# Token routing of a mixture-of-experts block: a written order for three engines, filler products, one product for the shift columns, and the last expert pairs without lag

## The chip, the cores and the metric

The kernel runs on one core of one Trainium2 chip. The metric is the device time of one execution in microseconds; the median of several runs is given. The engines that matter are TensorE (PE for products, PEld for its weight loads), VectorE (DVE), ScalarE (ACT), GpSimd (POOL) and SyncE (SP), which issues nearly all transfers from HBM.

## The reference, cut to what matters

The program computes one diffusion-transformer block (gated delta rule and dilated attention, then a mixture of experts) and two more layers (differential attention and a short convolution, each with an MLP) for 256 tokens of width 1024 in float32. The change touches the mixture of experts and what stands just ahead of it:

```python
h2 = _rms(x, g_ffn) * (1.0 + sc2) + sh2
scores = sigmoid(h2 @ w_router)                       # 256 x 64
sel = scores + router_bias
grp_score = sum of the two best sel of each of 8 groups; the 4 best groups stay
_, eidx = top_k(where(emask, sel, -inf), 8)           # 8 of 64 experts per token
wk = scores[eidx] / sum(scores[eidx]) * 2.5
routed = sum over experts e of (silu(h2 @ w_gate[e]) * (h2 @ w_up[e]) * wk[e]) @ w_down[e]
x = x + gt2 * (routed + shared expert)
```

Each expert has three weight arrays of 1 MB (1024x256, 1024x256, 256x1024); all 64 and the shared one are read.

## The kernel before

Phase A ends with the mixers' up-projections and w_out, whose output tiles arrive one 128-channel tile `f` at a time. `before_b` prepares what routing needs; among it the shift `sh2`, which lies as 8 columns of `self.mod` and is wanted in `self.shc` in another arrangement (channel p*8+j in row p, column j). It makes a row of 1024 values by 8 products with one column of weights (`ps_shr`, L904) and two copies on ScalarE (L905), and turns that row by 8 products with one row of weights (`ps_shc`, L909). `router` then splits the router weights and multiplies the shift with them (`ps_shl`, L923).

`ahead` runs once for each channel tile as soon as w_out has made it: a split in a rounded high part and a low part on ScalarE and VectorE (`xgh`, `xgl`), squares for the norm, then the router's products (`ps_r`) and transposes of the scaled tile (`ps_x`). `rows` follows the last tile: the norm factor `tr` (a power on GpSimd), the scores `th` (L1013), their tanh (L1015), and the token rows of h2 in high and low part, `h2th` (ScalarE, L1021) and `h2tl` (VectorE, L1022), four pieces each.

`route` finds each token's mask of 8 experts by a chain of VectorE instructions (`sel` L1031 to `mask` L1053) and ranks the tokens of each expert by products (`ps_rk`, L1059 and L1060). `order` counts tokens per expert, sorts experts by count (`key`, `rank`, `perm`), makes the list `ids` of experts in that order, the combine weights `cmb`, and `rks`/`cms`, ranks and weights in that order. The first 8 experts (N_FIX) are fixed, so the first pairs can start before the order is known.

Experts are worked off in "quads" of two units (a unit: two experts with 64 token slots each, or one with 128, or four with 32). For a quad, `places` makes one-hot matrices P on VectorE, `gather` makes the slots' inputs X from h2 (L1259, four steps, evicted by ScalarE at L1261), `weigh` makes the combine weights (L1275), `hidden` multiplies with gate and up weights (L1296), `gated` applies silu, `turned` transposes, `down` multiplies with the down weights (L1334), and `scatter` adds the result to the residual (L1349). The loop in `phase_b` runs these over 15 quads with a lag: in the turn of quad q it gathers q+1, multiplies q-1 with its down weights, and scatters q-2.

Weights come through SP into rings: 11 buffers of 1 MB in `ring2`, 4 in `ring`, and 3 in `ring4` for the start; a load waits until its buffer's last reader is done. Eighteen loads are issued ahead of routing.

The order of instructions on an engine comes from the planner of the language, by its own costs, except inside `tc.manual_schedule(engines=...)`: there the named engines keep the order of the program text. Before the change, only TensorE is so fixed, in the first gather and in the loop.

Of the kernel before, what the change touches and what calls it, by code (L numbers as in the profile page):

```python
# [10 lines left out]
F32 = mybir.dt.float32  # L11
# [7 lines left out]
T = 256  # L19
# [24 lines left out]
C_N = C_GRP + 24  # L44
B_SLOT, B_KEY, B_RANK, B_BASE, B_SH, B_MEM, B_COL, B_GRP = (
    c - C_SLOT for c in (C_SLOT, C_KEY, C_RANK, C_BASE, C_SH, C_MEM, C_COL, C_GRP))
# [22 lines left out]
N_WARM = 10  # L69


def make_consts():
# [44 lines left out]
class Kern:  # L117
# [231 lines left out]
    def phase_a(self):  # L349
        nc, tc, a, cst = self.nc, self.tc, self.a, self.cst  # L350
        with ExitStack() as st:
# [158 lines left out]
            for u in range(4):  # L510
                def sink(ft, ps, u=u):
                    f = u * 2 + ft
                    nc.vector.scalar_tensor_tensor(xT[:, f, :T], ps, gt[:, f:f + 1], xT[:, f, :T],
                                                   op0=ALU.mult, op1=ALU.add)
# [367 lines left out]
    def before_b(self):  # L882
# [78 lines left out]
    def ahead(self, j, sp):  # L961
# [6 lines left out]
        x = self.xT[:, j, :T]  # L968
        hi, lo = (sp.tile([128, T], F32R, tag=n, name=n, bufs=1) for n in ("xgh", "xgl"))
# [3 lines left out]
        sq = sp.tile([128, T], F32, tag="sqx" if j else "sqs", name="sqx", bufs=1)  # L973
        nc.scalar.activation(sq, x, AF.Square)
# [6 lines left out]
        yield  # L981

# [4 lines left out]
        if j == KC - 1:  # L987
# [1018 lines left out]
```

## Time and profile before

| | |
|---|---|
| median of 3 runs | 1699.44 us (1698.04 to 1704.7) |
| profiled execution, its own time | 1702.65 us |
| its span, first to last instruction | 1700.6 us |
| mean granted TensorE clock | 0.972 of full speed |
| TensorE busy | 1616.6 us, 95% of the span |
| VectorE, ScalarE, GpSimd busy | 956.6, 678.8, 136.4 us |
| HBM read | 388.85 MB |

Busy shares are averages over stages with different limits. The router's stage starts near 534 us of the span, the expert loop near 554, and the second block near 1039.

### The profile page before, as it was taken

How to read it: one execution, taken by the hardware profiler on the slowest of the kernel's cores; microseconds unless marked ns; L12 is line 12 of the kernel's file. 1: busy time of each engine (PE TensorE's matmuls, PEld its weight loads, DVE VectorE, ACT ScalarE, POOL GpSimd, SP SyncE). 2: the span in 40 equal slices, each digit the busy share in tenths (PEclk: the TensorE clock that was granted, in tenths of full speed). 3: DMA queues.
4: the chain of work that ended last, by engine and by line, in shares of the span. 5: the costliest groups of instructions: out<-in, count | busy, mean ns of one | idle time of the engine just before them, and what ended most of it. 6: DMA issues, size and time to landing. Idle time of an engine off the chain costs nothing. (4 is left out here: it accounts for less than half of the span.)

```text
span 1700.6 us, 31649 instructions
## 1 busy us (share of the span) xinstructions
PE 1616.6 (95%) x12857; PEld 1421.0 (84%) x12857; DVE 956.6 (56%) x2068; ACT 678.8 (40%) x1355; POOL 136.4 (8%) x120
## 2 busy tenths in 40 slices
PE   6999999999997999989999997999899999989998
PEld 3899999999997656756776655888899999989998
DVE  5779796976276132322243335675865447686543
ACT  4434334334444221222132213555554345465532
POOL 0121212122100000000000001011100010010000
PEclk8899999999998999999999998999899999989999
DMA  9535442555279599999999995423455554545552
GB/s 312 193 111 174 127 144 79 166 181 174 82 248 412 230 412 420 419 419 419 418 416 390 419 419 170 141 78 100 149 181 189 176 174 149 162 145 183 191 176 75
DMA packets 198496, 391.97 MB, mean 230 GB/s; under 512 B 8760, under 2 KB 158908, under 8 KB 173260
## 3 DMA queue, kind: packets, MB, share of 16 engines
q1 hardware_dynamic: 197916, 389.69, 62.9%
q8 instruction: 102, 1.67, 0.4%
q10 hardware_dynamic: 432, 0.23, 0.1%
q14 instruction: 46, 0.38, 0.1%
HBM read 388.85 MB, written 1.05 MB: 229 GB/s over the span
## 5 line engine op out<-in xcount | busy, mean ns | idle before, releaser
L148 ACT ACTIVATE hi<-w 128x1024 fp32r<-128x1024 f32 (+3 forms) x316 | 314.8, 1003 | 350.6 <-PE proj L167 248.7
L152 DVE TENSOR_TENSOR lo<-w,hi 128x1024 fp32r<-128x1024 f32 (+3 forms) x287 | 328.8, 1150 | 172.6 <-ACT hi L148 159.5
L1296 PE MATMUL ps_gu<-w,X 128*64 128x256 f32 (+2 forms) x2112 | 222.2, 388 | 11.9 <-DMA w<-in_w_exp_up 11.4
L1296 PEld LDWEIGHTS ps_gu<-w,X 128*64 128x64 f32 (+2 forms) x2112 | 145.7, 134 | 91.5 <-issue 16.0
L166 PE MATMUL proj<-hsh,hi 128*128 128x258 f32 (+2 forms) x824 | 208.5, 289 | 0.0
L167 PE MATMUL proj<-hsl,hi 128*128 128x258 f32 (+2 forms) x824 | 206.2, 285 | 0.0
L166 PE MATMUL proj<-hh,hi 128*128 128x256 f32 x640 | 168.2, 296 | 0.6 <-DVE cv L604 0.6
L167 PE MATMUL proj<-hl,hi 128*128 128x256 f32 x640 | 166.1, 292 | 0.1
L166 PEld LDWEIGHTS proj<-hsh,hi 128*128 128x128 f32 x824 | 156.9, 190 | 1.8 <-issue 1.1
L167 PEld LDWEIGHTS proj<-hsl,hi 128*128 128x128 f32 x824 | 157.7, 191 | 0.1
L152 POOL TENSOR_TENSOR lo<-w,hi 128x1024 fp32r<-128x1024 f32 x29 | 70.2, 2423 | 929.3 <-ACT hi L148 879.0
L1304 DVE SCALAR_TENSOR_TENSOR tg<-tg,ps_gu 128x256 f32<-128x256 f32 x30 | 12.6, 421 | 201.7 <-ACT tg L1303 201.7
L166 PEld LDWEIGHTS proj<-hh,hi 128*128 128x128 f32 x640 | 123.8, 193 | 1.9 <-issue 0.7
L167 PEld LDWEIGHTS proj<-hl,hi 128*128 128x128 f32 x640 | 123.6, 193 | 0.8 <-DVE hl L421 0.3
L169 PE MATMUL proj<-hsh,lo 128*128 128x258 f32 (+2 forms) x824 | 115.8, 283 | 0.0
L1334 PE MATMUL ps_d<-w,hT 128*64 128x512 f32 (+2 forms) x528 | 112.0, 597 | 0.7 <-DMA w<-in_w_exp_down 0.7
L169 PEld LDWEIGHTS proj<-hsh,lo 128*128 128x128 f32 x824 | 106.5, 189 | 0.0
L169 PE MATMUL proj<-hh,lo 128*128 128x256 f32 x640 | 102.8, 293 | 0.0
L1303 ACT ACTIVATE tg<-ps_gu 128x256 f32<-128x256 f32 x30 | 11.5, 384 | 215.8 <-PE ps_gu L1296 215.8
L166 PE MATMUL proj<-oh,hi 128*128 128x258 f32 (+1 forms) x384 | 96.2, 285 | 0.4 <-ACT oh L1939 0.4
L167 PE MATMUL proj<-ol,hi 128*128 128x258 f32 (+1 forms) x384 | 95.2, 283 | 0.0
L1334 PEld LDWEIGHTS ps_d<-w,hT 128*64 128x64 f32 (+2 forms) x528 | 34.4, 131 | 67.0 <-issue 46.2
(488 smaller groups left out, 3239.0 us busy)
## 6 DMA issues: line engine op xcount, KB each, us to landing
w<-in_w_in SPq DMA_DIRECT2D x66, 1024.0 KB, 5.1
w<-in_w_exp_up SPq DMA_DIRECT2D x64, 1024.0 KB, 17.7
w<-in_w_exp_gate SPq DMA_DIRECT2D x64, 1024.0 KB, 18.8
w<-in_w_exp_down SPq DMA_DIRECT2D x64, 1024.0 KB, 19.8
w<-in_w_up SPq DMA_DIRECT2D x32, 1024.0 KB, 5.5
w<-in_w_down SPq DMA_DIRECT2D x32, 1024.0 KB, 5.2
w<-in_w_ada SPq DMA_DIRECT2D x24, 1024.0 KB, 5.5
w<-in_w_out SPq DMA_DIRECT2D x8, 768.0 KB, 4.4
```

Source lines behind the costliest of these rows:

```text
L148: nc.scalar.activation(hi, v, AF.Copy)
L152: eng.tensor_tensor(lo, v, hi.bitcast(F32), op=ALU.subtract)
L166: nc.tensor.matmul(ps, wh(j), xh(j), start=(first and j == 0), stop=False)
L167: nc.tensor.matmul(ps, wh(j), xl(j), start=False, stop=False)
L169: self.last_mm = nc.tensor.matmul(ps, wl(j), xh(j), start=False, stop=(last and j == n - 1))
L1296: nc.tensor.matmul(ps[b0:b1, c * 256:c * 256 + 256], Q.X[:, j, n * 128 + b0:n * 128 + b1], w[:, j, :], start=(j == 0), stop=(j == KC - 1))
L1303: nc.scalar.activation(tg, ps[:, 0:256], AF.Tanh, scale=0.5)
L1304: nc.vector.scalar_tensor_tensor(tg, tg, 1.0, ps[:, 0:256], op0=ALU.add, op1=ALU.mult)
L1334: nc.tensor.matmul(psd[hf][b0:b1, :], hT[:, f, b0:b1], v[i][:, f, halves[hf]], start=(f == 0), stop=(f == 1))
```

## The change

It has five parts.

- **Shift columns by one product.** `before_b` multiplies, on VectorE, a constant pattern with the 8 shift columns (each broadcast over 16 columns) and turns the result by one product with a second constant pattern into `ps_shc`.
- **Written order of three engines.** `in_order` fixes TensorE, VectorE and ScalarE to the order of the text for the last channel tile, `rows`, `route`, the first steps of `order` and the first gather. That text is rearranged: squares and their products first in `ahead`; in `rows` the tanh after two of the four high parts, and only one of the four low parts there; two low parts ahead of `places` and one behind it.
- **Filler products.** Ten products of 128x128 with 128x256 into a bank that nothing reads, ahead of the ranking products.
- **Route in steps around gather.** `order` is a generator: its counting products come ahead of the places, its VectorE chain behind the first step of the gather, the `ids`, `sT` and `ps_end` products behind the gather, and the slot products behind the first `hidden`. `weigh` and `gated` of the first unit come ahead of the second `hidden`, `places` of the next quad too. In every turn `weigh` of the next quad now stands behind its `gather`, not between its steps. The banks of `pg` and `pgu` change sides with those of `pm`, `pd` and `py`; `PT` has 3 buffers in place of 4, `tg` one in place of 2.
- **Last pairs without lag.** In the turn before the last, the quad of that turn is turned, multiplied with its down weights, and its predecessor scattered, so that in the last turn only one scatter and the last quad's own work are left.

```diff
+    out[:, C_TURN:C_TURN + 128] = p // 8 == i % 16
+    out[:, C_TURN + 128:C_TURN + 136] = p % 8 == np.arange(8)[None, :]
...
                     f = u * 2 + ft
-                    nc.vector.scalar_tensor_tensor(xT[:, f, :T], ps, gt[:, f:f + 1], xT[:, f, :T], op0=ALU.mult, op1=ALU.add)
-                    yield from self.ahead(f, wk)
+                    with self.in_order(f == KC - 1):
+                        nc.vector.scalar_tensor_tensor(xT[:, f, :T], ps, gt[:, f:f + 1], xT[:, f, :T], op0=ALU.mult, op1=ALU.add)
+                        ahead = self.ahead(f, wk)
+                        next(ahead)
+                    yield
+                    with self.in_order(f == KC - 1):
+                        list(ahead)
...
-            self.rows()
+            with self.in_order():
+                self.rows()
+    def in_order(self, so=True):
+        E = mybir.EngineType
+        return self.tc.manual_schedule(engines={E.PE, E.DVE, E.Activation}) if so else nullcontext()
...
-        row = self.ring.tile([128, 2048], F32, tag="w", name="w")[0:1, 0:D]
-        for hf in range(2):
-            ps = self.pm.tile([128, 512], F32, tag="m", name="ps_shr")
-            for j in range(4):
-                c = 24 + hf * 4 + j
-                nc.tensor.matmul(ps[0:1, j * 128:j * 128 + 128], self.mod[:, c:c + 1], self.ident, start=True, stop=True)
-            nc.scalar.activation(row[:, hf * 512:hf * 512 + 512], ps[0:1, :], AF.Copy)
+        turn = self.ring.tile([128, 2048], F32, tag="w", name="w")[:, 0:128]
+        nc.vector.tensor_tensor(turn.rearrange("p (j i) -> p j i", j=8), self.CB[:, B_TURN:B_TURN + 128]...,
+                                self.mod[:, 24:32].unsqueeze(2).to_broadcast([128, 8, 16]), op=ALU.mult)
         ps = self.pm.tile([128, 512], F32, tag="m", name="ps_shc")
-        vs = row.rearrange("o (p j) -> o j p", j=KC)
-        for j in range(KC):
-            nc.tensor.matmul(ps[:, j:j + 1], vs[:, j, :], self.ones[0:1, 0:1], start=True, stop=True)
+        nc.tensor.matmul(ps[:, 0:KC], turn, self.CB[:, B_TURN + 128:B_TURN + 136], start=True, stop=True)
...
     def rows(self):
+        def part(n, lo): ...                      # one of the four pieces of h2th (lo False) or h2tl (lo True)
+        part(0, False)
+        part(1, False)
         nc.scalar.activation(self.th, self.th, AF.Tanh, scale=0.5)
-        for t in range(2):
-            for hf in range(2): ...               # h2th and h2tl, piece by piece
+        part(2, False)
+        part(3, False)
+        part(0, True)
+        self.low_parts = lambda ns: [part(n, True) for n in ns]
...
     def route(self, tok, sp):
+        psw = pm.tile([128, 512], F32, tag="m", name="ps_w")
+        for _ in range(N_IDLE):                   # 10
+            nc.tensor.matmul(psw[:, 0:256], self.ident, self.C[:, 0:256], start=True, stop=True)
...
     def phase_b(self):
+            with self.in_order():
+                psk = self.route(self.tok, self.sp)
+                order = self.order(self.tok, self.sp)
+                next(order)                       # counting products
+                first = self.quad(psk[:, :, E_FIX:], None, units[0:2], wk)
+                self.low_parts((1, 2))
                 self.places(first, self.slm)
-                list(self.gather(first))
-            self.order(self.tok, self.sp)
+                self.low_parts((3,))
+                gs = self.gather(first)
+                next(gs)
+                next(order)                       # rk, key, rank, perm, cmb, cmf, cnt, room, extra
+                list(gs)
+                next(order)                       # ps_ids, sT, ps_end
...
                     self.hidden(Q, 0)
-                    if q:
-                        self.gated(Q, 0)
+                    if q == 0:
+                        list(order)               # slot products, rks, cms
+                        list(self.weigh(Q))
+                    self.gated(Q, 0)
+                    if nxt:
+                        self.places(nxt)
+                    else:
+                        list(self.scatter([old.out[n] for n in range(2)]))
                     self.hidden(Q, 1)
+                    self.gated(Q, 1)
+                    if not nxt:
+                        break
                     for i in range(4):
                         next(ys, None)
-                        next(ws, None)
-                        next(gs, None)
                         if i > 1 and old:
                             self.turned(old, i - 2)
+                        next(gs)
                     list(ys)
                     list(gs)
                     list(ws)
                     if old:
                         self.down(old, 0, wo)
                         self.down(old, 1, wo)
-                for i in range(2):
-                    self.turned(Q, i)
-                list(self.scatter([old.out[n] for n in range(2)]))
+                    if q == nq - 2:
+                        for i in range(2):
+                            self.turned(Q, i)
+                        list(self.scatter([old.out[n] for n in range(2)]))
+                        self.down(Q, 0, wo)
+                        self.down(Q, 1, wo)
+                self.turned(Q, 0)
                 self.down(Q, 0, wo)
+                self.turned(Q, 1)
                 list(self.scatter([Q.out[0]]))
                 self.down(Q, 1, wo, True)
                 list(self.scatter([Q.out[1]]))
```

## Rows read from the trace of the kernel before

**Rows 1.** Windows of the expert stage: stretch, length, busy of each engine, clock, transfers.
```profile
553.50:561.50 8.00, 8.00 (x64) 5.14 (x65) 1.09 (x6) 1.62 (x5) 0.00 (x0) 1.00 0.08 19
...
575.50:585.50 10.00, 10.00 (x76) 8.07 (x78) 1.07 (x6) 2.74 (x7) 0.00 (x0) 0.83 0.06 13
585.50:1021.00 435.50, 421.25 (x3408) 281.30 (x3404) 139.19 (x352) 97.69 (x214) 0.00 (x0) 0.99 1.01 415
```

**Rows 2.** Timeline of SP's transfers: start, duration, queue, line, what.
```profile
560.12 0.80 SPq L1212 DMA_DIRECT2D w<-in_w_exp_down  x2
564.08 19.99 SPq L1212 DMA_DIRECT2D w<-in_w_exp_gate  x4
```

**Rows 3.** TensorE's waits from 600 to 985 us: total, times, longest.
```profile
PE ps_gu L1296 <- DMA w<-in_w_exp_up: 11.4, 9, 1.9
```

**Rows 4.** Timeline of 460 to 471 us: shift columns and first product behind.
```profile
460.57 1.91 PE L904 MATMUL ps_shr<-consts,mod 128*1 128x128 f32 x16
...
461.88 0.57 ACT L905 ACTIVATE w<-ps_shr 1x512 f32<-1x512 f32 x1
...
463.28 3.96 PE L909 MATMUL ps_shc<-consts,w 1*128 1x1 f32 x16 [0.80 <-ACT w L905]
...
466.11 1.65 ACT L148 ACTIVATE hi<-w 128x512 fp32r<-128x512 f32 x3
467.17 3.49 PEld L923 LDWEIGHTS ps_shl<-w,mod 128*128 128x128 f32 x16
...
470.61 0.56 PE L166 MATMUL proj<-ybh,hi 128*128 128x256 f32 x1
```

**Rows 5.** Windows as rows 1; the clock is the third number from the end.
```profile
467.00:473.00 6.00, 6.00 (x29) 5.99 (x29) 4.87 (x13) 1.06 (x3) 0.00 (x0) 0.50 0.39 128
...
537.00:544.70 7.70, 0.00 (x0) 0.00 (x0) 7.21 (x43) 2.10 (x5) 0.00 (x0) 0.57 1.01 417
```

**Rows 6.** Timeline of routing: VectorE and ScalarE from the factors to the first eviction.
```profile
536.45 2.42 ACT L1021 ACTIVATE h2th<-ps_x,tr 128x512 fp32r<-128x512 f32 x4 [1.16 <-POOL tr L230]
...
537.84 0.47 DVE L1013 SCALAR_TENSOR_TENSOR th<-ps_r,tr,shl 128x64 f32<-128x64 f32 x2
...
538.61 2.06 DVE L1022 SCALAR_TENSOR_TENSOR h2tl<-ps_x,tr,h2th 128x512 fp32r<-128x512 f32 x3
...
540.58 0.28 DVE L1031 SCALAR_TENSOR_TENSOR sel<-th,rb 128x128 f32<-128x128 f32 x1
...
544.46 0.23 DVE L1053 TENSOR_SCALAR mask<-rep 128x128 f32<-128x128 f32 x1
...
546.35 0.88 DVE L1248 TENSOR_TENSOR P<-slm,ps_rk 128x128 fp32r<-128x128 f32 x4 [0.52 <-PE ps_rk L1060]
...
547.87 0.22 ACT L1164 ACTIVATE cms<-cmb 128x16 fp32r<-128x16 f32 x1 [8.78 <-DVE cmb L1121]
...
549.29 0.84 ACT L1261 ACTIVATE X<-ps_g,shc 128x256 f32<-128x256 f32 x2 [1.20 <-PE ps_g L1259]
```

**Rows 7.** Timeline of the program's start: products of the fillers' shape.
```profile
32.14 4.88 PE L1528 MATMUL ps_w<-consts 128*128 128x256 f32 x12 [1.04 <-DVE mod L326]
```

**Rows 8.** Windows of the gather's products alone: PE busy (records), clock, transfers.
```profile
547.55:551.39 3.84, 3.84 (x19) 0.50 1.01 420
551.76:552.80 1.04, 1.04 (x11) 1.00 1.02 425
```

**Rows 9.** Timeline of TensorE in the first two pairs.
```profile
554.18 1.08 PE L1296 MATMUL ps_gu<-w,X 128*64 128x256 f32 x6
555.19 0.66 PE L1136 MATMUL ps_slots<-perm,sT 64*128 64x68 f32 x4
...
570.38 0.73 PE L1275 MATMUL ps_pt<-cms,P 128*128 128x256 f32 x4
...
580.04 14.03 PE L1296 MATMUL ps_gu<-w,X 128*64 128x256 f32 x128
```

**Rows 10.** TensorE's waits from 985 to 1040 us for weights.
```profile
PE ps_d L1334 <- DMA w<-in_w_exp_down: 0.7, 2, 0.4
```

More of the change, by code (lines that the diff above doesn't have):

```diff
@@ L1 @@
 import math
-from contextlib import ExitStack
+from contextlib import ExitStack, nullcontext
 from types import SimpleNamespace
@@ L69 @@
 N_WARM = 10
+N_IDLE = 10
 def make_consts():
@@ L968, in ahead @@
         x = self.xT[:, j, :T]
+        sq = sp.tile([128, T], F32, tag="sqx" if j else "sqs", name="sqx", bufs=1)
+        nc.scalar.activation(sq, x, AF.Square)
         hi, lo = (sp.tile([128, T], F32R, tag=n, name=n, bufs=1) for n in ("xgh", "xgl"))
@@ L991, in ahead @@
                     nc.tensor.matmul(self.ps_sq[:, t:t + 1], v[:, t * 128:t * 128 + 128], self.ones[:, 0:1], start=(n == 0), stop=(n == 1))
+        for t in range(2):
+            o, s = self.ps_r[t][:, 0:128], slice(t * 128, t * 128 + 128)
+            nc.tensor.matmul(o.rearrange("p (a b) -> p a b", a=2), hi[:, s], wr[:, :, j, :], start=(j == 0), stop=False)
+            nc.tensor.matmul(o[:, 0:64], lo[:, s], wr[:, 0, j, :], start=False, stop=(j == KC - 1))
         for t in range(2):
@@ L1089, in order @@
         nc.vector.tensor_scalar(perm, C[:E, B_RANK:B_RANK + 68], rank, None, op0=ALU.is_equal)
-        psi = pm.tile([128, 512], F32, tag="m", name="ps_ids")
-        nc.tensor.matmul(psi[0:1, 0:68], C[:E, B_COL + 1:B_COL + 2], perm, start=True, stop=True)
-        self.ids = tok.tile([1, 68], I32, name="ids", tag="ids")
-        nc.vector.tensor_copy(self.ids, psi[0:1, 0:68])
+        sc = sp.tile([128, 2, E], F32, tag="sc", name="sc", bufs=1)
+        nc.vector.tensor_scalar(sc, self.th, 0.5, 0.5, op0=ALU.mult, op1=ALU.add)
+        ws = small.tile([128, 2], F32, tag="wsum", name="wsum")
+        nc.vector.tensor_tensor(cmb, sc, mask, op=ALU.mult)
+        nc.vector.tensor_reduce(ws, cmb, axis=AX.X, op=ALU.add)
+        nc.vector.reciprocal(ws, ws)
+        for t in range(2):
+            nc.vector.tensor_scalar(cmb[:, t, :], cmb[:, t, :], ws[:, t:t + 1], 2.5, op0=ALU.mult, op1=ALU.mult)
+        self.dump("cmb", cmb)
+        self.dump("mask", mask)
+        self.cms, self.cmf = self.beside(tok, "cms", 72, N_FIX)
+        self.parts_of(cmb[:, :, E_FIX:], self.cmf)
         cnt = sp.tile([E, 1], F32, name="cnt", tag="cnt", bufs=1)
@@ L1106, in order @@
             nc.vector.scalar_tensor_tensor(ex, cnt, lim, ex, op0=ALU.is_gt, op1=ALU.add)
+        yield
+        psi = pm.tile([128, 512], F32, tag="m", name="ps_ids")
+        nc.tensor.matmul(psi[0:1, 0:68], C[:E, B_COL + 1:B_COL + 2], perm, start=True, stop=True)
+        self.ids = tok.tile([1, 68], I32, name="ids", tag="ids")
+        nc.vector.tensor_copy(self.ids, psi[0:1, 0:68])
+        self.rks = rks = tok.tile([128, 2, 72], F32, name="rks", tag="rks")
+        sTs = []
+        for src in (rk, cmb):
+            pst = pm.tile([128, 512], F32, tag="m", name="ps_sT")
+            for t in range(2):
+                nc.tensor.transpose(pst[:E, t * 128:t * 128 + 128], src[:, t, :], self.ident)
+            sTs.append(sp.tile([E, T], F32, tag="sT", name="sT", bufs=2))
+            nc.scalar.activation(sTs[-1], pst[:E, :T], AF.Copy)
         pse = pm.tile([128, 512], F32, tag="m", name="ps_end")
@@ L1114, in order @@
         nc.vector.tensor_copy(self.total, pse[:, 1:2])
[L1116 to L1133 removed]
+        yield
+        for src, sT in ((rk, sTs[0]), (cmb, sTs[1])):
             pss = pm.tile([128, 512], F32, tag="m", name="ps_slots")
@@ L1369, in phase_b @@
             wk = sb(px.enter_context, "wkx", "right", bufs=1)
-            psk = self.route(self.tok, self.sp)
             PE = {mybir.EngineType.PE}
-            first = self.quad(psk[:, :, E_FIX:], None, units[0:2], wk)
-            with tc.manual_schedule(engines=PE):
-                self.places(first, self.slm)
-                list(self.gather(first))
-            self.order(self.tok, self.sp)
-            self.sb4.close()
-            sm.close()
-            self.pd = sb(E2, "pd", "right", bufs=2, space=PSUM)
@@ L1382, in phase_b @@
             nq = len(units) // 2
-            quads = [self.quad(*((self.rks, self.cms) if 4 * q >= N_FIX else (self.rk[:, :, E_FIX:], self.cmf)),
-                               units[2 * q:2 * q + 2], wk) for q in range(nq)]
-            first.cmb = self.cmf
-            quads[0] = first
+            quads = [first]
             with tc.manual_schedule(engines=PE):
                 none = iter(())
-                for q, Q in enumerate(quads):
+                for q in range(nq):
+                    Q = quads[q]
+                    old = quads[q - 1] if q else None
@@ L1393, in phase_b @@
                     self.hidden(Q, 0)
-                    if q:
-                        self.gated(Q, 0)
+                    if q == 0:
+                        list(order)
+                        first.cmb = self.cmf
+                        quads += [self.quad(*((self.rks, self.cms) if 4 * q >= N_FIX else (self.rk[:, :, E_FIX:], self.cmf)),
+                                            units[2 * q:2 * q + 2], wk) for q in range(1, nq)]
+                        list(self.weigh(Q))
+                    self.gated(Q, 0)
```

82 lines of the change are left out of this document (29 added, 53 removed).

## The prediction, made before the result was known

> **What bounds the kernel now.** I read the profile from the transfers inwards. The stage that the change touches is the mixture of experts (450 to 1040 us of the span), and its windows show two regimes. From 585.5 to 1021 us the transfers run at 415 GB/s with a busy share of 1.01; ahead of that they stop twice: 19 GB/s from 553.5 to 561.5 and 13 GB/s from 575.5 to 585.5 [rows 1]. These two holes, some 18 us, are not a lack of work. SP issues a weight load when a ring buffer comes free: the next ones after the routing go out at 560.12 and 564.08, and the last of that group of four only near 584, when TensorE has used the buffers [rows 2]. So the start of the first two expert pairs sets when the stream restarts. Beyond 600 us TensorE is almost as full as the stream: from 600 to 985 it waits for gate and up weights some 11.4 us in 9 places, and hardly for anything else [rows 3]. Both clocks tick together there, so what starts earlier ends earlier by as much, if TensorE's own work per pair does not grow by more than that slack. Ahead of routing, to 534 us, TensorE's chain of dense products sets the time.
>
> **The shift columns (before_b).** Now 16 records (two for each of the 8 products) with one column of weights take 1.91 us from 460.57, two 0.57 us copies on ScalarE follow, and 16 records with one row of weights take 3.96 us; the next work, ps_shl, starts at 467.17 and the first product of w_up_dil at 470.61 [rows 4]. The change leaves one VectorE product, which can run long before, and one product of 8 columns (about 0.25 us, the pitch of the records just named). ps_shl can start near 460.8, 6.4 us earlier. That is not all gain: the first product also needs its hi part, which ScalarE starts at 466.11 at the end of an unbroken list [rows 4]. Without the two copies that is 464.97, with a copy of about 0.6 us the product starts at 465.6, 5.0 us earlier; the lo part on VectorE may then be late, for which I take off 0.5. The granted clock was 0.50 from 467 to 473, behind these thin products [rows 5]; whether it stays high with the short gap that is left is open. I take 4.5 us, with 2.5 (VectorE and a low clock) and 6 (the whole list moves) as ends. TensorE is full from there to 534 us, so it carries through.
>
> **Route, up to the gather.** The written order puts the four score steps th (two pairs of 0.47 us) ahead of the low parts of h2, the tanh behind two of the four h2th copies instead of four, and sel behind one low part instead of four. Now h2th starts at 536.45, th only at 537.84, three low parts (2.06 us) run from 538.61, and sel starts at 540.58 [rows 6]. In the new order: th 536.5 to 537.4, low part 0 to 538.1, tanh 537.7 to 538.0, sel at 538.1. From sel to the end of the mask is 4.1 us now, 0.2 less without sc: the mask ends at 542.1 in place of 544.69. Then two low parts (1.4 us) cover the ranking product, the places P take 0.88 [rows 6], the last low part 0.7. The gather can start at 544.5 and has all operands at 545.2, against 547.2 now.
>
> The ten fillers run on TensorE while it waits for the mask. Six like them took 4.88 us at the start of the program, 0.81 each, in part at the low clock [rows 7]; at the high level a record takes about half, as the gather's do (11 in 1.04 us at clock 1.00, 19 in 3.84 at 0.50) [rows 8]. So ten take 4.1 us at the high level and end before 541; at the low level 8.1 us, past the mask. Now TensorE does nothing from 537 to 544.7, the granted clock falls (0.57 in that stretch) [rows 5] and most of the gather runs at 0.50 [rows 8]. I take the fast level for the new gather: 32 products in 3.9 us in place of 6. The Trainium skill (TensorE: Matmul & The Clock Gate, What's actually happening) says that the throttled state is the default and activity releases it. The trace agrees; by that rule the fillers buy the fast gather and the sum below stands, and were only the gather's own products able to release the clock, it would be 8.5 us.
>
> Against the change speaks the order on ScalarE. The second step of order() ends its VectorE list with the combine weights, and their copy (cms, now at 547.87, waiting for cmb) is written between the evictions of gather pair 0 and pair 1. VectorE reaches cmb about 2.7 us after 545.1 (some 12 short steps of 0.2 to 0.3 us, as the rows of sel and the mask have them), so pair 1 is evicted at 548.1 and not at 547, 0.84 us each [rows 6]; pair 3 waits for its bank until 549.0 and the gather ends at 550 (now 553.1). The Trainium skill (the same page, Architectural detail) states that ScalarE and VectorE are strict FIFO, which is that cost; were the engine to pass the copy by, the gather would end at 549. The ids, sT and ps_end products took the 1.05 us up to the first hidden at 554.18 [rows 9]; with the second sT ahead of it I put 1.4 us: hidden starts at 551.4.
>
> **The first two pairs.** Now slot products cut into the first hidden, and the second ends at 570.4; then weights of the combine, places and gather fill 9.7 us until the next pair's hidden at 580.04 [rows 9]. In the new order hidden(0,0) is whole (7.0 us, half of a pair's 14.03), to 558.4; slots (two times 0.66) and weigh (0.73) with their hand-overs [rows 9] take 2.4; hidden(0,1) ends at 567.8; gather and weigh of the next pair take 5.3 (places done under hidden); hidden(1,0) starts at 573.1. That is 6.9 us earlier. The first buffers come free at 554.9 (now 560.1), the first hole shrinks from 8 to near 3 us, the second keeps its 9 to 10 but starts and ends earlier. Term: 7 us; 4 where the gather stays at the low clock (1.6 to 2 us) and another wait on an in-order engine comes in; 9 where no such queueing happens.
>
> **The loop.** weigh() of the next pair moves behind its gather. Its second bank is the one that the last gather eviction (0.84 us for two copies) [rows 6] must leave: about 0.75 us of idle TensorE in each of 13 pairs, 9.8 us. Before, other work lay in between. The slack of 11.4 us [rows 3] takes most of it, but lies mostly in the middle: I charge 2 us (0 to 6). PT with three buffers and tg with one cost nothing: the scatter that frees the oldest PT stands ahead of weigh, and two uses of tg lie a hidden (7 us) apart.
>
> **The tail.** The work of pair 13 moves ahead of the last pair. TensorE's waits for weights behind 985 us are 0.7 us [rows 10]; everything else there is its own work, and the same work remains. turned() right in front of down() now shows its copy on VectorE, some 0.4 us by the th and P rows. I take a gain of 1 us (a loss of 1 to a gain of 3).
>
> **Sum.** 4.5 + 7 + 1 - 2 = 10.5 us. The profiled execution took 1702.65 us (span 1700.6, 2.05 around it): 1692.1. The median shown is 1699.44, 3.2 us under it, so the forecast is 1689. The ends: 2.5 + 4 - 1 - 6 = a loss of 0.5, and 6 + 9 + 3 = a gain of 18: 1700 to 1681.
>
> **Rivals.** (1) *The gain is halved*: the fillers don't keep the clock, and waits written into the fixed orders of VectorE and ScalarE take what the better order gives; or the loop's idle of 0.75 us is not absorbed. For it: two slow stretches of the clock [rows 5] that follow thin TensorE work, and fillers leave over a microsecond idle behind them. Against it: the stretch becomes denser everywhere. With the low ends of route and loop, 4.5 + 4 + 1 - 6 = 3.5 us: 1696. Chance 0.28, with it all that ends within 0.5% (8.5 us, about what a measurement of this kernel tells from no change). (2) *TensorE becomes the bound of the loop, and the kernel slower*: the idle time in front of weigh's second bank is not 0.75 but 2.5 us, since the eviction stands in ScalarE's queue behind other copies. Thirteen pairs lose 32 us, 11.4 are absorbed, 12.5 gained elsewhere: 8.5 slower, 1708. It decides from (11.4 + 12.5) / 13 = 1.8 us a pair. Against it: 2.5 us would be three such evictions in a row, and weigh follows one. Chance 0.06. (3) *More is gained*: shift columns 6, route 9, tail 3: 1681. It is the upper part of the forecast, whose chance with it is 0.66.
>
> Faster by over 0.5%: 0.66, within: 0.28, slower: 0.06. The range that leaves out no more than 2 in 10: 1681 to 1699.
>
> **What would show it.** ps_shl starting 6 us behind the last product of the gates becomes under 1 us; sel starts under 2 us after the first h2th copy (now 4.1); the granted clock between 537 and 551 stays near 1.00; the two holes in the transfers sum to 11 to 13 us, not 18; hidden of the second pair 11 to 12 us earlier in the span; in the loop a wait of weigh's products for X of under 1 us a pair. Wrong it would be by a low clock in the gather, by a copy at the head of ScalarE's queue that waits longer than cmb, by a second hole that grows by what the first lost, or by a loop in which TensorE no longer waits for weights at all.

## The result, and the profile after

The changed kernel takes 1690.24 us (median of 9 runs, 1685.4 to 1694.95) where the kernel before takes 1699.44 (9 runs beside it, 1694.34 to 1704.88): a ratio of 0.9945, 95% interval 0.9927 to 0.9964. The forecast was 1689. The profiled execution took 1685.4 us with a span of 1683.3, the quickest of the nine, so the two profiles differ by 17.3 us where the medians differ by 9.2. To see what the change does, the span is cut into stages that start and end at the same instruction in every kernel (differences of starts and ends in the timelines):

- **S0**: from the first projection's first product to the first product of the shift columns. TensorE runs the same 3298 products there in every kernel here.
- **S1**: from there to the end of w_out's last product.
- **S2**: from there to the issue of expert load 24 (the first load is number 0), the first of the steady stream.
- **S3**: from there to the last expert load. **S4**: from there to the last addition to the residual.

| us | S0 | S1 | S2 | S3 | S4 | S1 to S4 |
|---|---|---|---|---|---|---|
| before | 422.9 | 72.9 | 50.8 | 418.5 | 35.7 | 577.9 |
| changed | 416.4 | 65.8 | 45.7 | 422.9 | 33.4 | 567.8 |

Of the 17.3 us, 6.6 stand in S0, where TensorE's work is unchanged, and 10.1 in the four stages that the change touches; the rest lies outside the five. They are three gains (7.1, 5.1 and 2.3) and a loss of 4.4 in the loop. Load 24, where S2 ends, is the first of these loads in the kernel before, and in the changed kernel:

```profile
584.30 6.67 SPq L1212 DMA_DIRECT2D w<-in_w_exp_up  x4
```

```profile
565.43 0.33 SPq L1243 DMA_DIRECT2D w<-in_w_exp_up  x1
```

The shift columns, in the timeline of the changed kernel (start, duration, engine, line, what; idle time in brackets), answer to [rows 4]:

```profile
452.94 1.12 PE L175 MATMUL proj<-hh,lo 128*128 128x256 f32 x8
...
453.89 0.28 PE L921 MATMUL ps_shc<-constb,w 128*128 128x8 f32 x2
454.04 1.98 PE L935 MATMUL ps_shl<-w,mod 128*128 128x64 f32 x16
...
455.82 0.48 PE L172 MATMUL proj<-ybh,hi 128*128 128x256 f32 x2
```

Two records make the columns where 32 thin ones stood; `ps_shl` starts 0.15 us behind them and takes 1.98 us at clock 1.00, where its weight loads alone took 3.49 at 0.50 [rows 4, 5]. ScalarE's timeline shows why the first product of w_up_dil need not wait:

```profile
439.95 0.63 ACT L931 ACTIVATE wr<-w 128x512 fp32r<-128x512 f32 x1 [2.86 <-DMA w<-in_w_router]
...
446.14 1.58 ACT L154 ACTIVATE hi<-w 128x512 fp32r<-128x512 f32 x2 [3.12 <-DMA w<-in_w_up_dil]
...
454.95 1.33 ACT L546 ACTIVATE ybh<-yb 128x256 fp32r<-128x256 f32 x4
```

The copies `wr` and `hi` are done between the gates' tanhs; before, they ran at 465 and 466 us, behind the row's two copies [rows 4].

The windows (length, busy time of five engines, then clock, share and rate of the transfers) answer to [rows 1, 5, 8]:

```profile
453.00:459.00 6.00, 6.00 (x51) 5.79 (x50) 4.14 (x13) 5.11 (x16) 0.00 (x0) 1.00 0.79 253
...
524.30:530.30 6.00, 6.00 (x22) 5.05 (x23) 5.49 (x37) 1.42 (x3) 0.00 (x0) 0.75 1.01 419
532.50:538.10 5.60, 5.53 (x40) 4.53 (x40) 4.09 (x26) 2.51 (x7) 0.00 (x0) 1.00 1.01 420
...
540.00:543.50 3.50, 3.50 (x36) 2.33 (x34) 0.00 (x0) 0.00 (x0) 0.00 (x0) 1.00 0.24 44
558.00:566.00 8.00, 7.56 (x66) 5.44 (x66) 1.17 (x8) 2.82 (x8) 0.00 (x0) 1.00 0.12 19
566.00:1006.50 440.50, 425.38 (x3424) 282.02 (x3422) 140.24 (x353) 96.69 (x215) 0.00 (x0) 1.00 1.00 411
```

Behind the shift columns the granted clock stays at 1.00 (0.50 before). It is 0.75 on average under the fillers and 1.00 in the gather. The two holes in the transfers are 3.5 and 8 us long, not 8 and 10; the stream behind them runs at 411 GB/s, not 415.

The routing, in the timeline, answers to [rows 6]:

```profile
524.28 6.04 PE L1079 MATMUL ps_w<-consts 128*128 128x256 f32 x20 [1.21 <-DVE th L1025]
...
524.71 0.28 DVE L1052 SCALAR_TENSOR_TENSOR sel<-th,rb 128x128 f32<-128x128 f32 x1
...
528.58 0.23 DVE L1074 TENSOR_SCALAR mask<-rep 128x128 f32<-128x128 f32 x1
528.73 1.40 DVE L1034 SCALAR_TENSOR_TENSOR h2tl<-ps_x,tr,h2th 128x512 fp32r<-128x512 f32 x2
...
530.16 0.33 PE L1085 MATMUL ps_rk<-mask,constb 128*128 128x64 f32 x2
...
530.98 0.88 DVE L1279 TENSOR_TENSOR P<-slm,ps_rk 128x128 fp32r<-128x128 f32 x4 [0.84 <-PE ps_rk L1085]
...
535.19 0.22 ACT L1195 ACTIVATE cms<-cmb 128x16 fp32r<-128x16 f32 x1 [0.51 <-DVE cmb L1123]
535.31 1.55 ACT L1292 ACTIVATE X<-ps_g,shc 128x256 f32<-128x256 f32 x4
```

`sel` comes 1.9 us after the first h2th copy at 522.81, and the mask ends 9.1 us behind w_out (11.2 before). But the fillers did not start when TensorE fell idle: the trace puts 1.2 us of wait in front of them down to `th`, a VectorE instruction that reads the pool of banks that theirs replaces. In a bank of the old pool they start 1.3 us earlier (early fillers, below). Here they start late, run half the time at the low clock, end at 530.3, 1.5 us behind the mask, and the ranking products and P wait for them.

The first two pairs on TensorE answer to [rows 9]:

```profile
539.30 6.69 PE L1327 MATMUL ps_gu<-w,X 128*64 128x256 f32 x58
545.92 1.11 PE L1167 MATMUL ps_slots<-perm,sT 64*128 64x68 f32 x8
547.74 0.73 PE L1306 MATMUL ps_pt<-cms,P 128*128 128x256 f32 x4 [0.71 <-DVE cms L1196]
548.40 7.13 PE L1327 MATMUL ps_gu<-w,X 128*64 128x256 f32 x64
...
561.16 14.03 PE L1327 MATMUL ps_gu<-w,X 128*64 128x256 f32 x128
```

The first `hidden` is no longer cut up, and the next pair's starts 41.5 us behind w_out where it was 46.6.

TensorE's waits from 583 to 968 us answer to [rows 3]:

```profile
PE ps_gu L1327 <- DMA w<-in_w_exp_up: 6.6, 5, 1.9
PE ps_pt L1306 <- ACT X L1292: 3.9, 12, 0.3
```

The waits for weights have shrunk from 11.4 us to 6.6, and weigh's products wait for the gather's evictions instead.

### The profile page after: what moved, and what is told of

It is laid out like the page before. It is cut to its first block, busy times and chain, and to the rows that moved or that the text cites. A ratio compares the mean times of both kernels' runs of the same rounds, so it can differ in the third digit from the quotient of the medians.

```text
span 1683.3 us, 31624 instructions
## 1 busy us (share of the span) xinstructions
PE 1604.9 (95%) x12847; PEld 1406.0 (84%) x12847; DVE 960.0 (57%) x2069; ACT 676.1 (40%) x1353; POOL 135.9 (8%) x120
## 5 line engine op out<-in xcount | busy, mean ns | idle before, releaser
L1327 PE MATMUL ps_gu<-w,X 128*64 128x256 f32 (+2 forms) x2112 | 218.7, 384 | 7.3 <-DMA w<-in_w_exp_up 6.6
L1334 ACT ACTIVATE tg<-ps_gu 128x256 f32<-128x256 f32 x30 | 11.5, 385 | 213.7 <-PE ps_gu L1327 213.7
## 6 DMA issues: line engine op xcount, KB each, us to landing
w<-in_w_exp_gate SPq DMA_DIRECT2D x64, 1024.0 KB, 16.3
```

Of the source, the lines that this page charges most:

```text
L1327: nc.tensor.matmul(ps[b0:b1, c * 256:c * 256 + 256], Q.X[:, j, n * 128 + b0:n * 128 + b1], w[:, j, :], start=(j == 0), stop=(j == KC - 1))
```

## The experiments

Medians and ratios are over 4 to 9 runs each, beside the kernel before on the same chip, whose medians were 1701.9 to 1702.5 there.

| kernel | median us | ratio, 95% interval | S0 | S1 | S2 | S3 | S4 |
|---|---|---|---|---|---|---|---|
| columns alone | 1695.62 | 0.9965, 0.9953 to 0.9978 | 424.4 | 65.7 | 49.7 | 418.5 | 35.7 |
| no fillers | 1691.37 | 0.9939, 0.9925 to 0.9954 | 424.5 | 65.8 | 47.4 | 423.0 | 33.4 |
| weigh between the steps | 1686.86 | 0.9918, 0.9903 to 0.9933 | 418.6 | 65.8 | 47.0 | 418.6 | 33.6 |
| old lag | 1693.49 | 0.9961, 0.9948 to 0.9974 | 418.3 | 65.8 | 46.9 | 422.1 | 35.7 |
| early fillers | 1691.39 | 0.9938, 0.9919 to 0.9957 | 417.3 | 65.8 | 44.9 | 422.9 | 33.4 |
| cms late | 1693.05 | 0.9953, 0.9941 to 0.9965 | 422.1 | 65.8 | 46.0 | 423.0 | 33.4 |
| TensorE's order alone | 1691.10 | 0.9941, 0.9924 to 0.9958 | 418.5 | 65.8 | 45.7 | 423.1 | 33.4 |
| weigh, 13 early fillers | 1686.19 | 0.9906, 0.9892 to 0.9921 | 417.0 | 65.8 | 47.3 | 418.7 | 33.5 |
| three edits | 1688.07 | 0.9916, 0.9902 to 0.9930 | 423.4 | 65.8 | 46.5 | 418.6 | 33.5 |
| three edits, bridge | 1681.03 | 0.9880, 0.9865 to 0.9896 | 418.3 | 65.8 | 44.1 | 418.6 | 33.5 |
| three edits, no fillers | 1686.41 | 0.9920, 0.9899 to 0.9941 | 418.1 | 65.8 | 46.3 | 418.6 | 33.5 |
| changed, again | 1689.14 | 0.9926, 0.9911 to 0.9941 | 423.0 | 65.8 | 45.9 | 423.0 | 33.4 |

S1, S3 and S4 repeat to 0.2 us wherever their code is the same. S2 and above all S0 don't, so a median is trusted for some 3 us, and a stage is read from the trace.

**Columns alone** (the kernel before with the new `before_b`).

```diff
...
-        row = self.ring.tile(...)   # 8 products ps_shr, 2 copies, 8 products ps_shc
+        turn = self.ring.tile([128, 2048], F32, tag="w", name="w")[:, 0:128]
+        nc.vector.tensor_tensor(turn..., pattern, self.mod[:, 24:32]..., op=ALU.mult)
+        nc.tensor.matmul(ps[:, 0:KC], turn, self.CB[:, B_TURN + 128:B_TURN + 136], start=True, stop=True)
```

> The kernel before with the shift columns alone changed. From the last product of the gates to the first product of w_up_dil the kernel before needs 10.1 us and the changed one 1.9 us. Theory A (the columns are the main part of the gain, more than I forecast, since TensorE's clock no longer falls behind thin products): that stretch takes about 2 us here, the granted clock stays at 1.00 there, TensorE is full from there to the end of w_out, so the last product of w_out comes 7 to 8 us earlier and the time is 1692 us. Rival (the columns bring the 4.5 us that I forecast; the larger difference between the two profiles is an accident of the clock or needs the written order): the stretch takes 5 to 6 us, the clock falls again, 1695 us. A third possibility: the first part of the expert stage is bound by its transfers and takes the gain back: 1698 us.

The stretch is 1.93 us, S1 is 65.7 as in the changed kernel, and the time falls by 0.35% (6 us). TensorE's timeline of this run:

```profile
463.12 0.28 PE L907 MATMUL ps_shc<-constb,w 128*128 128x8 f32 x2
463.26 1.98 PE L921 MATMUL ps_shl<-w,mod 128*128 128x64 f32 x16
```

Theory A: the columns are worth 7.2 us by themselves, without a written order. S2 is the code of before here and 1.2 us shorter (49.7 for 50.8). The granted clock tells why: it is 1.00 from 549 to 578 us in this run, while in the profile of the kernel before it was 0.83 on average from 575.5 to 585.5 us [rows 1], under the gather of the second pair. So up to 1.2 of the 5.1 us that S2 gains are the clock of one profile.

**No fillers, and early ones.**

```diff
-N_IDLE = 10
+N_IDLE = 0
```

> The changed kernel without the ten filler products. Theory A (they hold TensorE's clock, but come too late: in the changed kernel they wait for th, end at 530.3 us, behind the mask, and hold up the ranking product and with it P by 0.8 us): without them P starts 0.8 us earlier after the mask, the clock in the gather is near 0.5, and its 32 products take about 6 us instead of 3.9, so that the first hidden starts about 1 us later than now: 1691 us. Rival 1 (the fillers are what makes the gather fast, nothing else): the gather takes 2 to 3 us longer, the first pair's start moves by as much, 1693 us. Rival 2 (the gather waits for ScalarE's evictions at either clock, the fillers only delay): first hidden 0.8 us earlier, 1689.5 us.

```diff
 def ahead(self, j, sp):                       # behind the last transposes
+        if j == KC - 1:
+            psw = self.pp.tile([128, 512], F32, tag="proj", name="ps_w")
+            for _ in range(N_IDLE):
+                nc.tensor.matmul(psw[:, 0:256], self.ident, self.C[:, 0:256], start=True, stop=True)
...
 def route(self, tok, sp):
-        psw = pm.tile(...)                        # the same products, ahead of ps_rk
```

> The changed kernel with its ten fillers moved forward: behind the last transposes of ahead, into a bank of the old pool pp that is free by then, so that they don't wait for th. Counted from the end of the last w_out product, the start of P and the issue of load 24 stand at 12.9 and 50.8 us in the kernel before, 11.3 and 45.7 in the changed one, 12.5 and 46.9 in the run with the old lag (same routing, the fillers took 7 us at the low clock there), 10.8 and 47.3 without fillers. Theory A (the fillers are right but late: the clock falls while they wait for th, and then they hold up the ranking): they start 1.2 us earlier, still at the high clock, take 4.1 us, end before the mask; P stands at 10.5 to 10.8, the gather runs at clock 1.00, load 24 at 45.0 to 45.5, and the time is about 1.5 us under the changed kernel's 1690.2, 1688.7. Rival (in the 1.6 us that are left open up to the mask the clock falls again): P at 10.8, but a gather like the one without fillers, load 24 at 47 us, 1690.5 us.

Without fillers P stands at 10.8 us behind w_out (11.3 with them), the gather runs mostly at 0.50, and S2 is 1.7 us longer than the changed kernel's: the mechanism of theory A, with a loss between it and rival 1. Early ones give the shortest S2 of the single edits, 44.9, where theory A had 45.0 to 45.5: they end 9.37 us behind w_out, just as the ranking starts (9.42). Yet they took 6.06 us and not 4.1, since the clock fell to 0.50 under them too. Neither median can be told from the changed kernel's. In the run with the old lag, same routing, the fillers took 6.99 us, P came at 12.5, and S2 was 46.9. Against the one profile without them, the changed kernel's fillers bring between 0.5 and 1.7 us of S2, by where the clock happens to fall, and early ones 2.5.

Behind the early fillers TensorE stood idle for the low parts, and the clock was at 1.00 before, in and after that gap (timeline, then windows):

```profile
523.65 6.06 PE L1009 MATMUL ps_w<-consts 128*128 128x256 f32 x20
...
532.42 0.38 PE L1290 MATMUL ps_g<-P,h2th 128*128 128x256 f32 x1 [1.21 <-DVE h2tl L1038]
```

```profile
530.35:531.35 1.00, 0.86 (x11) 0.70 (x10) 1.00 (x4) 0.00 (x0) 0.00 (x0) 1.00 1.08 451
531.35:532.35 1.00, 0.00 (x0) 0.00 (x0) 1.00 (x4) 0.00 (x0) 0.00 (x0) 1.00 1.04 434
532.35:533.35 1.00, 0.93 (x8) 0.93 (x8) 0.90 (x7) 0.00 (x0) 0.00 (x0) 1.00 0.97 401
```

**TensorE's order alone.**

```diff
-        return self.tc.manual_schedule(engines={E.PE, E.DVE, E.Activation}) if so else nullcontext()
+        return self.tc.manual_schedule(engines={E.PE}) if so else nullcontext()
```

> The changed kernel in which only TensorE keeps the written order in the routing; VectorE and ScalarE are ordered by the planner as in the kernel before. From the end of the last w_out product to the end of the mask the kernel before needs 11.2 us, the changed one 9.1; sel follows the first h2th copy by 4.1 and 1.9 us. Theory A (the order of VectorE and ScalarE is what makes the mask earlier): the stretch takes 10.5 to 11.5 us, load 24 comes 1.5 to 2 us later, 1692 us. Rival (the text is rearranged, and the planner finds the same order from it): 9 to 9.5 us, 1690 us.

The mask comes at 11.1 us, as theory A has it, but S2 is 45.7 and the time 1691.1: no loss. The fillers ended at 12.2 us behind w_out here and hid the later mask, and the gather's first product, at 13.6, lay inside the 12.9 to 14.1 of the kernels that have all three orders and the same fillers. Besides, the planner lets VectorE begin the combine weights (`cmb`) at 533.75 us, ahead of P at 535.46, so that ScalarE's cms copy between the first evictions has nothing to wait for: from the gather's first product to load 24 it is 32.1 us here, 32.9 in the changed kernel. Written order on VectorE and ScalarE saves 2 us up to the mask; late fillers and the wait of that copy (next run) spend it.

**cms late.**

```diff
 def order(self, tok, sp):
-        self.parts_of(cmb[:, :, E_FIX:], self.cmf)      # ahead of cnt
...
         yield                                           # behind the gather
+        self.parts_of(cmb[:, :, E_FIX:], self.cmf)
```

> The changed kernel with the copy and the remainder of the first pairs' combine weights (cms) written behind the gather, not between its first and second step. The prediction charged this copy 1 us: it stands between the evictions of gather pairs 0 and 1 on ScalarE and waits for VectorE's list. In the changed kernel's trace ScalarE idles 0.51 us in front of it, and TensorE fills the wait for the bank with six products of the first hidden. Theory A (the wait is covered by those six products, so it costs almost nothing): the second eviction starts 0.5 us earlier, the issue of load 24 stays within 0.3 us of the changed kernel's, the time within 1 us, 1690 us. Rival (the queue on ScalarE holds up the first pair): first hidden and load 24 come 1 us earlier, 1689 us.

ScalarE in this run:

```profile
540.97 1.77 ACT L1291 ACTIVATE X<-ps_g,shc 128x256 f32<-128x256 f32 x4 [8.66 <-PE ps_g L1289]
543.11 1.77 ACT L1291 ACTIVATE X<-ps_g,shc 128x256 f32<-128x256 f32 x4 [0.36 <-PE ps_g L1289]
544.77 0.21 ACT L1194 ACTIVATE cms<-cmb 128x16 fp32r<-128x16 f32 x1
```

The first two evictions run back to back. From the gather's first product to load 24 it is 32.1 us, 32.9 in the changed kernel (32.8 with the old lag, 32.9 with weigh between the steps): the rival is right on the stage, and the copy in ScalarE's queue costs 0.8 us. This agrees with the strict FIFO of the Trainium skill (TensorE: Matmul & The Clock Gate, Architectural detail). In the time it drowns: this run's fillers ended at 11.7 us.

**Weigh between the gather's steps.**

```diff
-        Q.PT = Q.wk.tile([128, len(Q.units), T], F32R, tag="PT", name="PT", bufs=3)
+        Q.PT = (Q.wk2.tile([128, len(Q.units), T], F32R, tag="PT", name="PT", bufs=4) if Q.wk2 is not Q.wk
+                else Q.wk.tile([128, len(Q.units), T], F32R, tag="PT0", name="PT0"))
...
                         next(ys, None)
-                        if i > 1 and old:
-                            self.turned(old, i - 2)
+                        next(ws, None)
                         next(gs)
+                        if i > 1 and old:
+                            self.turned(old, i - 2)
```

> The changed kernel with weigh of the next quad between the steps of its gather, as in the kernel before (one PT buffer more). In the changed kernel TensorE waits in the loop 3.9 us in 12 places for X in front of weigh's products, and the stretch from load 24 to the last load takes 423.5 us against 418.6 before. Theory A (that wait, where TensorE and not the stream sets the time, is what the loop loses): the waits for X vanish, the stretch is 2 to 4 us shorter, 1687 us. Rival (the stretch is set by the transfers, which have less stall ahead of it and therefore more to do at once): waits vanish, stretch and time the same within 1 us, 1690 us.

Theory A: S3 is 418.6 again, 4.3 us shorter, and the median 3 us lower. The buffers of PT were changed along with the order and not tried alone; the idle time in the changed kernel's row below is put down to X, not to PT. The group of weigh's products (line, what, count, busy and mean ns, idle ahead of them) from load 24 to the last, first in the changed kernel and then in this run:

```profile
L1306 PE MATMUL ps_pt<-cms,P 128*128 128x256 f32 x52 | 13.0, 331 | 5.8 <-ACT X L1292 4.6
```

```profile
L1307 PE MATMUL ps_pt<-cms,P 128*128 128x256 f32 x52 | 10.5, 283 | 0.0
```

Behind the gather they cost 5.8 us of idle time and 2.5 us more of their own; the waits for weights in front of `hidden` pay less than half of it back, as the waits for up weights of this run (6.6 in the changed kernel) show:

```profile
PE ps_gu L1328 <- DMA w<-in_w_exp_up: 10.6, 8, 1.9
```

**Old lag in the last two turns.**

```diff
...
-                    if q == nq - 2:
-                        for i in range(2):
-                            self.turned(Q, i)
-                        list(self.scatter([old.out[n] for n in range(2)]))
-                        self.down(Q, 0, wo)
-                        self.down(Q, 1, wo)
-                self.turned(Q, 0)
+                for i in range(2):                # behind the last turn, as in the kernel before
+                    self.turned(Q, i)
+                list(self.scatter([old.out[n] for n in range(2)]))
                 self.down(Q, 0, wo)
-                self.turned(Q, 1)
```

> The changed kernel with the old lag in the last two turns. From the issue of the last expert load to the last addition to the residual the kernel before takes 35.7 us, the changed one 33.4. Theory A (the last pairs without lag are worth these 2.3 us): the stretch takes 35.5 to 36 us here, 1692.5 us. Rival (the difference comes from where the stream stood when the last load was issued, not from the order): the stretch takes 33.5 us with the old lag too, 1690 us.

S4 is 35.7, as theory A has it. But the old lag also shortens S3, by 0.8 us (422.1 for 422.9). At load 183, 407.6 us behind load 24, the two kernels are still level; load 185 then goes out at 411.1 us here and at 415.9 in the changed kernel, whose turn before the last holds more work. S3 and S4 together are 457.8 us here and 456.3 there: the last pairs without lag are worth 1.5 us, and 3.6 of the 4.4 us lost in S3 are the loop's.

**Combinations.** Weigh between the steps with thirteen early fillers, the three edits together (weigh, ten early fillers, cms late), the same with two more fillers ahead of the gather, and without any:

```diff
 def order(self, tok, sp):                     # behind the counting products
+        psw = pm.tile([128, 512], F32, tag="m", name="ps_w")
+        for _ in range(2):
+            nc.tensor.matmul(psw[:, 0:256], self.ident, self.C[:, 0:256], start=True, stop=True)
         yield
```

> The changed kernel with weigh between the gather's steps, as in the run before that measured 1686.9 us, and with thirteen fillers moved forward as in the run with early fillers. Theory A (the two losses are independent, and thirteen products of 0.41 us reach to the mask without passing it): stretch from load 24 to the last load 418.6 us as in the first of the two, load 24 at 45.0 to 45.5 us behind the last w_out product: 1685.3 us. Rival (the earlier start of the first pairs meets the same stream of transfers and is lost in it): 1687 us.

> The changed kernel with three edits that earlier runs tried singly: weigh between the gather's steps, the ten fillers behind the last transposes, the cms copy behind the gather. Theory A (they act at different places and add up): from the last w_out product to the issue of load 24 about 44.1 us (44.9 with early fillers alone, less 0.8 for the copy), load 24 to the last load 418.6 us, 1684 us. Rival (a TensorE clock that falls by chance in the routing makes 1 to 2 us of it): load 24 at 45 to 46.5 us, 1685.5 us.

> As the run with the three edits, and two more filler products between the counting products and the gather, where TensorE stands idle 1.1 us for the low parts; with thirteen early fillers the granted clock fell to 0.50 in the gather, which then took 6.8 us. Theory A (that idle time is what lets the clock fall in the gather): the gather runs at 1.00 throughout, load 24 at 44 us, 1684 us. Rival (the two products only delay the gather, or the clock falls all the same): load 24 0.5 to 1 us later, 1685 us.

> As the run with the three edits, without any filler product. Theory A (the fillers save 1 to 2 us by the clock in the gather when they don't delay the ranking): mask as early, gather mostly at clock 0.50, load 24 at 46 to 46.5 us, 1686 us. Rival (the gather at the low clock is hidden behind its evictions once the copy is out of the way): load 24 at 44.5 us, 1684.5 us.

S3 is 418.6 or 418.7 in all four. S2 fell short of theory A in the first two (47.3 and 46.5), both times with a low clock in the gather; the thirteen fillers also ended 1.6 us behind the mask. Of the run with the three edits, TensorE, and the windows of the fillers and the gather:

```profile
529.73 4.48 PE L1009 MATMUL ps_w<-consts 128*128 128x256 f32 x20
535.78 0.41 PE L1085 MATMUL ps_rk<-mask,constb 128*128 128x64 f32 x2 [1.56 <-DVE mask L1078]
...
538.45 0.58 PE L1289 MATMUL ps_g<-P,h2th 128*128 128x256 f32 x1 [1.27 <-DVE h2tl L1038]
```

```profile
529.70:534.20 4.50, 4.50 (x22) 3.65 (x20) 3.86 (x31) 2.67 (x5) 0.00 (x0) 1.00 1.02 426
538.40:545.20 6.80, 6.75 (x33) 6.61 (x34) 3.89 (x24) 2.52 (x6) 0.00 (x0) 0.54 1.02 422
```

Here the fillers did what I had priced: high clock, 4.48 us (4.1 priced), done ahead of the mask. Then TensorE stood idle twice, for the mask and for the low parts, the clock fell to 0.54 on average in the gather, and S2 is no better than without fillers (46.5 and 46.3). So that last run gives theory A's numbers (46.3 us, 1686.4) but not its reading: these fillers, which did not delay the ranking, saved nothing. With the bridge:

```profile
525.71 6.10 PE L1009 MATMUL ps_w<-consts 128*128 128x256 f32 x20
...
533.24 1.13 PE L1105 MATMUL ps_w<-consts 128*128 128x256 f32 x4
534.48 0.39 PE L1292 MATMUL ps_g<-P,h2th 128*128 128x256 f32 x1
```

```profile
534.40:538.80 4.40, 4.32 (x34) 3.98 (x34) 3.91 (x25) 2.52 (x6) 0.00 (x0) 1.00 1.02 423
```

The gather runs at 1.00 and ends 16.3 us behind w_out, 2.4 us ahead of the run without the bridge; S2 is 44.1, as theory A has it. This is the fastest kernel of the study, 1681.03 us, 1.2% under the kernel before. Its median lies 7.0 us under that of the run without the bridge, but of the difference between their profiles only 2.4 us stand in S2, and 5.0 in S0, where the code is the same. That the two products keep the clock up fits this one profile, but the run with early fillers speaks against it. There, too, the fillers fell to the low clock and ended only at the mask; TensorE then stood idle for 1.21 us with no bridge, and the gather ran at 1.00 all the same. It started 12.07 us behind w_out, 12.03 with the bridge, and S2 was 0.8 us longer, which is the price of the copy. So no run shows a gain of the bridge by itself. The run with the three edits lost its clock in the second of its two idle times (1.56 and 1.27 us); with fillers at the high clock the bridge was not seen.

**The changed kernel once more.**

> The changed kernel once more, unchanged, for its profile. Theory A (the two profiles shown differ by 6.6 us ahead of the change's place, in the same instructions, only because the granted clock fell at other places): this profile's end of the gates' products stands elsewhere than 416.4 us behind the first projection, somewhere between 416 and 425 us, and the stages behind it last as in the first profile: 65.8 us from there to the last w_out product, 45.7 to 47 to load 24, 423 to the last load. Rival (the changed kernel is laid out otherwise and runs its first half faster each time): 416 to 417 us again. The time is 1690 to 1692 us by either.

Theory A: S0 is 423.0 this time, and the four stages sum to 568.1 us, against 567.8.

## Why the prediction was right

By the four stages the change brings 10.1 us in one profile of the changed kernel and 9.9 in the other, against 10.5 in the sum, and most signs named beforehand are there (`ps_shl` at the end of the gates' last product, `sel` 1.9 us behind the first h2th copy, holes of 11.5 us together, waits for X of 0.3 us at most). One is there by half: the clock was 1.00 in the gather, but 0.75 under the fillers. No term has the size that I gave it: by stages 7.1 for 4.5, 5.1 for 7, 2.3 for 1, a loss of 4.4 for 2. The errors (+2.6, -1.9, +1.3, -2.4) cancel to -0.4, which was luck. With the tail and the loop parted as the run with the old lag does it (1.5 and 3.6) the sum is the same.

- **Shift columns.** Mis-sized, beyond my upper end of 6, which was meant for a list that moves as a whole. The step that failed is the start of the hi part "at the end of an unbroken list": I kept ScalarE's list and only shortened it by the two copies. Without a copy that waits for TensorE, the `wr` and `hi` copies moved ahead by 19 and 13 us, counted from the first product of the columns; the first product came 8.1 us earlier (1.93 for 10.04), the clock stayed at 1.00, and one wait of 1.3 us for `thb` on VectorE gave a part back. What made the planner move them was not tried by itself.
- **Route and first two pairs.** The mask, 2.1 us earlier, was priced at 2.6, and the copy in ScalarE's queue at 1 (0.8 measured). The failing step is that the fillers take 4.1 us at the high level and end before 541: they waited for `th`, ran half the time at the low clock and ended 1.5 us behind the mask. So the gather started 12.9 us behind w_out, not 11.7, and the next pair's hidden came 41.5 us behind w_out and not 39.6. Of these missing 1.9 us the late gather is 1.1, the gather and weigh of the next pair are 0.3 (5.6 us where I had 5.3), and the rest lies in small parts between. In the bridged run, where neither fillers nor copy are in the way, the gather starts at 12.0 us and ends at 16.3 (16.5 in the sum, which has 1 us for the copy), and the stage has gained 6.7 us of my 7. Against the columns-alone run, whose second pair met no low clock, the gains are 3.9 and 5.5 us: part of the term was the clock of the profile that I started from.
- **The clock.** The fast gather came as forecast in the changed kernel, 1.00, where the windows of the gather have 0.62 to 0.65 in two runs without fillers. This is in line with the rule of the Trainium skill (TensorE: Matmul & The Clock Gate, What's actually happening) that activity releases it. But ten fillers did not hold it in the run with the three edits (0.54), and where nothing else hid it, it was worth about 2 us of S2 (46.5 and 46.3 against 44.1).
- **The loop.** The price a pair was right: (5.8 + 2.5) / 13 = 0.64 us where I had 0.75. The slack was the mistake: I let 11.4 us of waits for weights absorb all but 2 us. They absorbed 3.7 (waits for up and gate weights: 11.1 in the run with weigh between the steps, 7.4 in the changed kernel); the other pairs lie where TensorE is full without a wait, such as 845 to 905 us in the kernel before, busy 60.00 of 60.00. Slack counts only in the pairs that have it.
- **The tail.** Right in sign, and near in size: S4 gains 2.3 us, S3 pays 0.8 of them, which leaves 1.5 for 1.
- **The rivals.** TensorE did not become slower by 1.8 us a pair but by 0.64, far from the second rival's point. Of the first, all causes occurred in part: the route, with its late fillers at a low clock, fell 1.9 us short of its term, and the loop, by stages, cost 2.4 us more than I charged. These 4.3 of the rival's 7 us were made up by the columns and the tail (+3.9), the luck named above.

## What to carry to other kernels

A copy that waits for one engine at the head of another's list can cost more than itself (here 0.22 us long, 0.8 lost), and when such copies go, look for what can then move forward, not only at their duration (4.5 us priced, 7.2 measured). Slack absorbs a new cost only in the turns of the loop in which it lies, so set the cost of each turn against the wait of the same turn. Filler products brought 0.5 to 1.7 us here although they came late, 2.5 us when they ended at the mask, and nothing when the clock fell behind them: check what makes them late (their own operands and banks), and read their worth from more than one profile. The end of a stage can move with the edit that is tried in the next one, so add the stages on both sides of the border before you put a price on it.

## What the runs showed of the hardware

The granted clock falls at different places in executions of the same instructions. Over the fourteen profiles S0 takes between 416.4 and 424.5 us; the mean granted clock over S0 is 1.00 where the changed kernel takes 416.4 us and 0.98 where it takes 423.0. The window from 66 to 72 us, first of the changed kernel and then of the same kernel again:

```profile
66.00:72.00 6.00, 5.54 (x48) 5.30 (x47) 4.32 (x12) 2.79 (x6) 2.30 (x4) 1.00 0.19 52
```

```profile
66.00:72.00 6.00, 6.00 (x30) 6.00 (x29) 1.26 (x5) 1.47 (x2) 0.80 (x1) 0.50 0.00 0
```

The clock is 1.00 in one and 0.50 in the other, with 48 and 30 products done. That is as large as most single edits here, and two profiles can't be subtracted as wholes: the stages that hold the same code have to be taken out first.
